# One DMA queue for the stores, and row loads issued a step ahead, in a projection, RWKV-7 and FFN kernel

## The chip, the cores and the metric

The kernel runs on one core of one Trainium2 chip. The metric is the device time of an execution in microseconds, as the median of several runs. The engines are named as the profile names them: PE (matmul), PEld (weight load, beside PE), DVE (vector), ACT (scalar), POOL (GpSimd) and SP (sync, which only issues transfers here). SPq, ACTq and POOLq are the sequencers of these engines where they issue transfers.

## The reference, cut to what matters

One layer over 2048 frames of width 1024, all in float32:

```
h = rms_norm(x);  z = h @ w_in                        # 3328 columns
y_conv = b * conv3(c * x_in)                          # from 12 x 128 columns of z
y_rwkv = rwkv7(token_shift_lerp(z[rwkv columns]))     # 8 heads of 64, chunks of 64 frames
x = x + concat(y_conv, y_rwkv) @ w_out
x = x + (silu(gate) * val) @ w_down                   # gate, val: conv3(rms_norm(x) @ w_up) + bias
e = rms_norm(p @ w_proj)
x = x + sigmoid(rms_norm(x) @ w_gate) * e
out = rms_norm(x)
```

## The kernel before, in words

Features lie on the partitions and time on the free axis. The 2048 frames are worked in four groups of 512. Every product is split in float32r parts (hi and lo of the rows, hi and lo of the weights) and takes three matmuls of 128x512 for each block of 128 features.

The dense stream has two parts. First come the input projections of all four groups (`in_proj`): for each group 14 products whose results go through the token-shift lerp to a DRAM tensor `zs`, then 12 for the convolution mixer, whose results go to `ys`. After that, each group goes through `dense_rest`: the output projection (`w_out`, tiles `whlo`), up projections in pairs with their convolution (`whlu`, `uf`, `th`), down projections (`ps_d`), the embedding of `p` (`ple_embed`, results to DRAM as `es`), and eight gate products (`whlg`), each of which reads one row of `es` back (`e`). While a group is in its convolution mixer, rows `x` of the next group are loaded and split; in its gate products, rows `y` of the next group are.

Beside the dense stream runs `rwkv`, a generator over 16 units of 128 frames. `drive` takes one step of it for about each half product of the dense stream, so its matmuls lie between the dense ones. A unit first loads its inputs from `zs` (`rwkv_load`: k, tw, ad, gd, v, r). In its middle it sends a block matrix through DRAM (`ltt` to `ld` to `lm`), solves a triangular system on DVE (`pd`, `xs`), and sends the result through DRAM again (`xs` to `xd` to `dt`), from which DVE makes `dn` and POOL fills `tT`. At its end it stores `yt` to `ys`.

Weights are loaded raw in the first pass only (SP loads, tile `raw` with four buffers, split by ACT and POOL, kept in DRAM by an SP store); in later passes POOL loads the split form. Rows from DRAM go through staging tiles with tag `s` (three buffers). Most results of 128x512 share tag `b` (`buf`, six buffers), which a store holds until it has landed.

PE keeps the order of the program. On the other engines a scheduler lists the instructions, and each engine then works through its list in order: an instruction or a transfer that waits holds up all behind it.

Of the kernel before, what the change touches and what calls it, by code (L numbers as in the profile page):

```python
# [24 lines left out]
R_POST = 3  # L25
R_SCORE = 3
# [4 lines left out]
WRAW = 4  # L31
WHL = 4
NBUF = 6
NLD = 3
# [28 lines left out]
def tile_trunk(  # L63
# [226 lines left out]
    def in_row(pools, g, rows, k):  # L290
        with tc.high_priority():
            x = staged(pools, xT[k, :, g * G : (g + 1) * G], "x")
        rows.add(pools, x, v("mix_norm_g", k))

    def in_proj(pools, g, rows, nxt):
# [18 lines left out]
        for i in range(4):  # L314
# [17 lines left out]
            def evac_b(ps, rstd):  # L332
                u = buf(pools, "yc")
                nc.vector.tensor_tensor(out=u, in0=ps, in1=rstd, op=ALU.mult)
                nc.vector.tensor_tensor(out=u, in0=u, in1=st["c"], op=ALU.mult)
                nc.scalar.dma_start(out=ys[g][:, i, :], in_=u)
# [11 lines left out]
    def ple_rows(pools, g):  # L348
        hs = []
        with tc.high_priority():  # L350
            for k in range(2):
                hi, lo = pair(pools)
                t = staged(pools, pT[k, :, g * G : (g + 1) * G], "p")
# [25 lines left out]
    def out_row(pools, g, rows, k):  # L379
        rows.ss = None  # L380
        with tc.high_priority():
            hi, lo = pair(pools)
            t = staged(pools, ys[g][:, k, :], "y")
# [3 lines left out]
    def dense_rest(pools, g, yrows, nxt):  # L387
# [77 lines left out]
        for first in range(0, NFF, NB):  # L465
            acts = []
            for i in range(first, min(first + NB, NFF)):
                if i == first + 2 and prev is not None:
                    yield from down(first - NB, prev)
                yield from act_pair(i, acts)  # L470
                if i == PLE_AT - 1:
                    prows = ple_rows(pools, g)
# [10 lines left out]
        re = embed[g]  # L483
        for m in range(KD):
# [22 lines left out]
            for _ in product(pools, w, rows3, evac):  # L507
                yield SLOW

        def finish():  # L510
            rstd = ss.rstd(pools)
            with tc.high_priority():
                for m in range(KD):
# [5 lines left out]
                    nc.scalar.dma_start(out=out[m, :, gs], in_=t)  # L519
# [33 lines left out]
    def rwkv_load(rp, S, u):  # L553
# [14 lines left out]
        nc.sync.dma_start(out=r_t, in_=zs[g][:, 0:4, ts])  # L568
        kkv = v("rwkv_k_k", 0, 4)[:, :, None].broadcast_to([P, 4, P])
# [5 lines left out]
        return r_t, k_t, v_t, gd, kr, sq  # L575

    def rwkv_unit(rp, S, u, loaded, following):
# [188 lines left out]
        for pq in range(4):  # L766
            q = pq % 2
            nc.scalar.dma_start(
# [4 lines left out]
        for r in range(4):  # L773
            eng = nc.sync if r % 2 else nc.scalar
# [33 lines left out]
        for pq in range(4):  # L808
            eng = nc.sync if pq % 2 else nc.scalar
# [19 lines left out]
        yield from rest(WAIT - R_BONUS)  # L829
# [101 lines left out]
        nc.scalar.dma_start(out=ys[g][:, 4:8, ts], in_=yt)  # L931
# [18 lines left out]
    def rwkv():  # L950
        following = [None]
        for u in range(4 * NG):
            loaded = following[0] or rwkv_load(rp, S, u)
# [6 lines left out]

    def in_next(g):
        def run(k):
            if g < NG and k < KD:
                in_row(pools, g, rows["in", g], k)
# [24 lines left out]
    for k in range(KD):  # L989
# [11 lines left out]
    for k in range(KD):  # L1001
# [72 lines left out]
```

## Time and profile before

| | |
|---|---|
| median of 3 runs | 2907.62 us (2907.26 to 2908.49) |
| the profiled execution | 2908.45 us |
| its span | 2906.5 us |
| PE busy | 2768.1 us (95%) |
| DVE, POOL, ACT busy | 1908.3, 1117.4 and 959.9 us |
| mean granted clock of PE | 0.984 |

The span is the time from the first to the last instruction of the profiled execution; about 2 us of its time lie outside. Matmuls overlap their neighbours, so that a busy PE is not a PE without loss; idle PE time is loss for certain.

### The profile page before, as it was taken

How to read it: one execution, taken by the hardware profiler on the slowest of the kernel's cores; microseconds unless marked ns; L12 is line 12 of the kernel's file. 1: busy time of each engine (PE TensorE's matmuls, PEld its weight loads, DVE VectorE, ACT ScalarE, POOL GpSimd, SP SyncE). 2: the span in 40 equal slices, each digit the busy share in tenths (PEclk: the TensorE clock that was granted, in tenths of full speed). 3: DMA queues.
4: the chain of work that ended last, by engine and by line, in shares of the span. 5: the costliest groups of instructions: out<-in, count | busy, mean ns of one | idle time of the engine just before them, and what ended most of it. 6: DMA issues, size and time to landing. Idle time of an engine off the chain costs nothing.

```text
span 2906.5 us, 42153 instructions
## 1 busy us (share of the span) xinstructions
PE 2768.1 (95%) x15464; PEld 2226.7 (77%) x15464; DVE 1908.3 (66%) x3039; ACT 959.9 (33%) x1721; POOL 1117.4 (38%) x1700
## 2 busy tenths in 40 slices
PE   8999999999889999989999999999999999999997
PEld 5778888778677877767778887777788877788885
DVE  5575665648587868796766676857676765544446
ACT  5332232312553433443412223434222143411113
POOL 4533232324556565652333333333333332433221
PEclk9999999999999999989999999999999999999998
DMA  8887777767777777767666565766565668666665
GB/s 298 297 261 217 236 214 223 209 210 243 263 252 245 258 241 247 248 228 230 178 186 185 173 192 172 233 202 200 174 192 169 187 187 266 216 195 189 196 188 169
DMA packets 285802, 629.95 MB, mean 217 GB/s; under 512 B 60186, under 2 KB 113690, under 8 KB 285596
## 3 DMA queue, kind: packets, MB, share of 16 engines
q0 software_dynamic: 95040, 346.07, 39.4%
q1 hardware_dynamic: 134144, 232.83, 24.0%
q10 hardware_dynamic: 56412, 48.36, 5.2%
q8 instruction: 122, 2.00, 0.3%
q14 instruction: 84, 0.69, 0.1%
HBM read 467.77 MB, written 159.38 MB: 216 GB/s over the span
## 4 chain that ended last, share of the span: by engine, by line
PE 50%; DVE 22%; DMA 14%; issue 6%; ACT 5%; POOL 3%; ACTq 1%; SPq 0%; DVEq 0%; POOLq 0%
PE ps_mm L86 33%; PE ps_d L86 11%; DVE uf L417 3%; DVE pd L794 3%; DVE xs L798 2%; DMA lm<-ld 1%; DMA xd<-xs 1%; DMA ld<-ltt 1%; DVE zb L255 1%; DVE sq L229 1%; DMA es<-e 1%; PE o_ps L86 1%; DMA dt<-xd 1%; DVE lo L215 1%; DMA x<-in_xT 1%
## 5 line engine op out<-in xcount | busy, mean ns | idle before, releaser
L86 PE MATMUL ps_mm<-hi,whlu 128*128 128x512 f32 x2816 | 910.6, 397 | 11.3 <-POOL whlu L154 5.1
L86 PEld LDWEIGHTS ps_mm<-hi,whlu 128*128 128x128 f32 x2816 | 532.3, 189 | 131.9 <-POOL whlu L154 7.8
L86 PE MATMUL ps_mm<-hi,whlin 128*128 128x512 f32 x1664 | 542.9, 400 | 19.6 <-ACT whlin L153 7.1
L86 PE MATMUL ps_mm<-lo,whlu 128*128 128x512 f32 x1408 | 552.3, 392 | 1.5 <-DVE lo L215 1.5
L86 PE MATMUL ps_d<-hi,whld 128*128 128x512 f32 x1408 | 456.1, 396 | 16.7 <-DMA whld<-kd 7.2
L86 PEld LDWEIGHTS ps_mm<-hi,whlin 128*128 128x128 f32 x1664 | 316.7, 190 | 93.0 <-ACT whlin L153 7.1
L417 DVE SCALAR_TENSOR_TENSOR uf<-zb,vec,uf 128x512 f32<-128x512 f32 x352 | 298.6, 851 | 89.6 <-ACT uf L412 78.4
L86 PE MATMUL ps_mm<-lo,whlin 128*128 128x512 f32 x832 | 328.9, 395 | 2.8 <-DVE lo L215 2.8
L412 ACT ACTIVATE uf<-zb,vec 128x512 f32<-128x512 f32 x176 | 143.1, 815 | 562.0 <-DVE zb L255 536.8
L86 PEld LDWEIGHTS ps_d<-hi,whld 128*128 128x128 f32 x1408 | 265.6, 189 | 79.2 <-DVE x L457 8.4
L86 PEld LDWEIGHTS ps_mm<-lo,whlu 128*128 128x128 f32 x1408 | 266.8, 189 | 56.2 <-DVE lo L215 2.4
L161 POOL DMA_DIRECT2D whlu<-ku x264 | 141.7, 537 | 436.8 <-PE ps_mm L86 289.1
L255 DVE TENSOR_TENSOR zb<-ps_mm,rstd 128x512 f32<-128x512 f32 x216 | 148.5, 688 | 208.0 <-PE ps_mm L86 204.4
L86 PE MATMUL ps_d<-lo,whld 128*128 128x512 f32 x704 | 275.4, 391 | 0.0
L457 DVE TENSOR_TENSOR x<-ps_d,x 128x512 f32<-128x512 f32 x192 | 131.6, 687 | 139.5 <-PE ps_d L86 138.7
L86 PEld LDWEIGHTS ps_mm<-lo,whlin 128*128 128x128 f32 x832 | 158.4, 190 | 38.1 <-DVE lo L215 6.6
L161 POOL DMA_DIRECT2D whlin<-kin x156 | 84.1, 539 | 248.9 <-PE ps_mm L86 207.7
L86 PE MATMUL ps_mm<-hi,whlg 128*128 128x512 f32 x512 | 169.2, 406 | 3.4 <-DMA whlg<-kg 3.4
L86 PE MATMUL ps_mm<-hi,whlo 128*128 128x512 f32 x512 | 163.1, 397 | 8.5 <-DMA whlo<-ko 4.9
L154 POOL TENSOR_TENSOR lo<-th,hi 128x512 fp32r<-128x512 f32 x88 | 115.2, 1310 | 110.9 <-ACT hi L153 110.3
L154 POOL TENSOR_TENSOR whlu<-rawu,whlu 128x512 fp32r<-128x512 f32 x88 | 122.6, 1398 | 88.9 <-ACT whlu L153 79.2
L86 PEld LDWEIGHTS ps_d<-lo,whld 128*128 128x128 f32 x704 | 133.2, 189 | 26.0
(205 smaller groups left out, 4248.0 us busy)
## 6 DMA issues: line engine op xcount, KB each, us to landing
whlu<-ku POOLq DMA_DIRECT2D x264, 512.0 KB, 4.5
whlin<-kin POOLq DMA_DIRECT2D x156, 512.0 KB, 4.8
whld<-kd POOLq DMA_DIRECT2D x132, 512.0 KB, 4.0
ku<-whlu SPq DMA_DIRECT2D x88, 512.0 KB, 4.7
kin<-whlin SPq DMA_DIRECT2D x52, 512.0 KB, 5.3
whlo<-ko POOLq DMA_DIRECT2D x48, 512.0 KB, 5.5
whlg<-kg POOLq DMA_DIRECT2D x48, 512.0 KB, 3.9
rawu<-in_w_up SPq DMA_DIRECT2D x88, 256.0 KB, 4.1
```

Source lines behind the costliest of these rows:

```text
L86: return pin(nc.tensor.matmul(*args, **kw))
L154: nc.gpsimd.tensor_tensor(out=lo, in0=raw, in1=hi.bitcast(F32), op=ALU.subtract)
L161: nc.gpsimd.dma_start(out=t, in_=kept[key])
L215: nc.vector.scalar_tensor_tensor(out=lo, in0=src, scalar=gcol, in1=hi.bitcast(F32), op0=ALU.mult, op1=ALU.subtract)
L229: nc.vector.tensor_tensor(out=sq, in0=sq, in1=self.acc, op=ALU.add)
L255: nc.vector.tensor_tensor(out=zb[:, 2 : G + 2], in0=ps, in1=rstd, op=ALU.mult)
L412: nc.scalar.activation(u, zb[:, 2 : G + 2], AF.Identity, bias=v("ffn_conv_b", n), scale=v("ffn_conv_w", 88 + n),)
L417: nc.vector.scalar_tensor_tensor(out=u, in0=zb[:, d : d + G], scalar=v("ffn_conv_w", 44 * d + n), in1=u, op0=ALU.mult, op1=ALU.add,)
L457: nc.vector.tensor_tensor(out=x2[m], in0=ps, in1=x2[m], op=ALU.add)
L794: tt(out=pd[:, :, :, 0:n], in0=xs[:, :, None, 0:n].broadcast_to([P, 8, 2, n]), in1=lm[:, None, i : i + 2, 0:n].broadcast_to([P, 8, 2, n]), ...
L798: nc.vector.tensor_reduce(out=xs[:, :, i : i + 2], in_=pd[:, :, :, 0:n], op=ALU.add, axis=mybir.AxisListType.X,)
```

## The change

All stores that ACT issued (`zs`, `ys`, `es`, `out`, `ld`) and its halves of `lm` and `dt` are issued by SP: 280 transfers. The load of a row is split from its first use, which comes one call of `nxt` later (`x`, `y`), one feed-forward pair later (`p`), or half a product later (`e`). `rwkv_load` only issues loads; `rwkv_first` holds the first operations and stands six steps later. Unit 0 starts two steps later. There are four staging tiles, and three raw weight tiles where there were four.

```diff
 R_POST = 3
+R_LOAD = 6
...
-WRAW = 4
+WRAW = 3
...
-NLD = 3
+NLD = 4
...
-    def in_row(pools, g, rows, k):
+    def in_load(pools, g, k):
         with tc.high_priority():
-            x = staged(pools, xT[k, :, g * G : (g + 1) * G], "x")
+            return staged(pools, xT[k, :, g * G : (g + 1) * G], "x")
+
+    def in_row(pools, rows, k, x):
         rows.add(pools, x, v("mix_norm_g", k))
...
-                nc.scalar.dma_start(out=zs[g][:, j, :], in_=u)
+                nc.sync.dma_start(out=zs[g][:, j, :], in_=u)
...
-                    nc.scalar.dma_start(out=es[g][:, m, :], in_=t)
+                    nc.sync.dma_start(out=es[g][:, m, :], in_=t)
...
+        ahead = e_load(0)
         for m in range(KD):
             nxt(m)
             w = weight(pools, w_gate[m], f"g{m}")
+            e = ahead
             with tc.high_priority():
-                e = staged(pools, es[g][:, m, :], "e")
                 nc.vector.tensor_tensor(out=e, in0=e, in1=re, op=ALU.mult)
...
+            steps = product(pools, w, rows3, evac)
+            next(steps)
+            yield SLOW
+            if m + 1 < KD:
+                ahead = e_load(m + 1)
+            for _ in steps:
                 yield SLOW
+        nxt(KD)
...
-            nc.scalar.dma_start(
+            nc.sync.dma_start(
                 out=ld[pq].rearrange("c a i j -> i c a j"),
...
-            eng = nc.sync if r % 2 else nc.scalar
+            eng = nc.sync
...
-            eng = nc.sync if pq % 2 else nc.scalar
+            eng = nc.sync
...
-        yield from rest(WAIT - R_BONUS)
+        yield from rest(R_LOAD)
+        if following[0]:
+            rwkv_first(S, following[0])
+        yield from rest(WAIT - R_BONUS - R_LOAD)
...
     def rwkv():
-        following = [None]
+        following = [rwkv_load(rp, S, 0)]
+        yield from rest(R_BONUS)
+        rwkv_first(S, following[0])
+        yield from rest(R_BONUS)
...
         def run(k):
             if g < NG:
-                while k >= 4 and marks["done"] < 4 * g + 3:
-                    next(side, None)
-                out_row(pools, g, rows["out", g], k)
+                if k < KD:
+                    while k >= 4 and marks["done"] < 4 * g + 3:
+                        next(side, None)
+                    loads["out", g, k] = out_load(pools, g, k)
+                if k:
+                    out_row(pools, rows["out", g], k - 1, loads.pop(("out", g, k - 1)))
```

How the lists of the engines move at three places. First ACT in the embedding of group 1's `p`, where `e` is a product's result, `sq` its square, and `tw`, `s` and `tha` are the RWKV unit's. Before:

```order
L370 COPY e<-ps_e 128x512
L619 ACTIVATE tha_13168<-ps_a 128x512
L227 ACTIVATE sq<-e 128x512
L371 DMA es_103<-e 128x512
L370 COPY e<-ps_e 128x512
L572 ACTIVATE tw_144<-tw_144 64x128
L227 ACTIVATE sq<-e 128x512
L371 DMA es_103<-e 128x512
L370 COPY e<-ps_e 128x512
L227 ACTIVATE sq<-e 128x512
```

The same place after the change:

```order
L376 COPY e<-ps_e 128x512
L228 ACTIVATE sq<-e 128x512
L376 COPY e<-ps_e 128x512
L228 ACTIVATE sq<-e 128x512
L376 COPY e<-ps_e 128x512
L639 ACTIVATE s_13216<-ps_s 128x512
L228 ACTIVATE sq<-e 128x512
L645 ACTIVATE tha_13224<-ps_a 128x512
L599 ACTIVATE tw_144<-tw_144 64x128
L661 COPY nrd_13252<-ksum_13248 64x4 x4
```

The stores are gone from ACT, and the unit's `tha` and `tw` stand behind all eight `e` instead of among them; `tw` still comes right behind `tha`.

Second SP at the end of the gate products of group 0 and the start of group 1's output projection (`xr` are its residual rows, `kg` stores of kept weights). Before:

```order
L203 DMA e<-es_102 128x512
L171 DMA kg_1_12205<-whlg_1_12200 128x1024
L203 DMA y<-ys_99 128x512
L203 DMA e<-es_102 128x512
L171 DMA kg_0_12254<-whlg_0_12249 128x1024
L203 DMA y<-ys_99 128x512
L775 DMA lm_12036<-ld_12029 32x1024 x2
L203 DMA e<-es_102 128x512
L171 DMA kg_1_12261<-whlg_1_12256 128x1024
L203 DMA xr<-in_xT 128x512 x8
```

After:

```order
L204 DMA e<-es_102 128x512
L204 DMA y<-ys_99 128x512
L172 DMA kg_0_12247<-whlg_0_12242 128x1024
L172 DMA kg_1_12254<-whlg_1_12249 128x1024
L204 DMA e<-es_102 128x512
L204 DMA y<-ys_99 128x512
L204 DMA xr<-in_xT 128x512
L794 DMA ld_12117<-ltt_12118 32x8x32 x4
L204 DMA xr<-in_xT 128x512 x2
L801 DMA lm_12124<-ld_12117 32x1024 x4
L204 DMA xr<-in_xT 128x512 x3
L541 DMA out<-o 128x512 x5
```

The last `e` and `y` come ahead of the unit's `lm`; `ld` and all four `lm` now stand among the residual rows, and the output stores of the group before behind six of them.

Third SP in the lerp products of group 2, which fill `zs_96`. Before, SP had only the unit's transfers there:

```order
L564 DMA tw_144<-zs_95 64x128
L565 DMA ad_146<-zs_95 64x128
L566 DMA gd_5097<-zs_95 128x128
L203 DMA y<-ys_98 128x512
L563 DMA k_5093<-zs_95 128x4x128
L567 DMA v_5094<-zs_95 128x4x128
L568 DMA r_5092<-zs_95 128x4x128
L775 DMA lm_5018<-ld_5011 32x1024 x2
L803 DMA xd_5079<-xs_5029 128x256
L810 DMA dt_5081<-xd_5079 32x8x32 x2
```

After, for the unit at this place:

```order
L588 DMA gd_3918<-zs_94 128x128
L311 DMA zs_96<-u 128x512
L585 DMA k_3914<-zs_94 128x4x128
L589 DMA v_3915<-zs_94 128x4x128
L590 DMA r_3913<-zs_94 128x4x128
L311 DMA zs_96<-u 128x512 x3
L794 DMA ld_3832<-ltt_3833 32x8x32 x4
L801 DMA lm_3839<-ld_3832 32x1024 x3
L311 DMA zs_96<-u 128x512
L801 DMA lm_3839<-ld_3832 32x1024
L311 DMA zs_96<-u 128x512 x4
L829 DMA xd_3900<-xs_3850 128x256
```

The stores of the lerp results stand behind the unit's `ld` and `lm`, each of which waits for the step before it.

## Rows read from the trace of the kernel before

**Rows 1.** The page: span, busy time of PE, granted clock in 40 slices.
```profile
span 2906.5 us, 42153 instructions
...
PE 2768.1 (95%) x15464; PEld 2226.7 (77%) x15464; DVE 1908.3 (66%) x3039; ACT 959.9 (33%) x1721; POOL 1117.4 (38%) x1700
...
PEclk9999999999999999989999999999999999999998
```
**Rows 2.** Windows, PE alone: stretch, length, busy (instructions), clock, DMA share, GB/s.
```profile
100.00:120.00 20.00, 15.90 (x78) 0.91 0.70 246
...
755.00:1205.00 450.00, 419.86 (x2556) 0.98 0.72 247
1205.00:1312.00 107.00, 93.01 (x470) 0.89 0.68 225
...
1400.00:1425.00 25.00, 22.51 (x108) 0.93 0.80 240
...
1800.00:1906.00 106.00, 100.25 (x461) 0.97 0.76 241
...
1965.00:1985.00 20.00, 16.92 (x83) 0.91 0.85 258
...
2365.00:2445.00 80.00, 74.70 (x313) 0.96 0.76 234
...
2530.00:2840.00 310.00, 309.17 (x1365) 1.00 0.65 193
2840.00:2907.00 67.00, 47.13 (x198) 0.88 0.50 158
```
**Rows 3.** Timeline of PE at the first RWKV unit; in brackets idle time and releaser.
```profile
109.88 0.66 PE L89 MATMUL ps_n<-c_sq,sq 128*128 128x128 f32 x4 [2.04 <-ACT sq L571]
112.59 1.09 PE L89 MATMUL ps_v<-c_sq,v 128*128 128x128 f32 x4 [2.05 <-DMA v<-zs]
```
**Rows 4.** Timeline of ACT, POOL and PE at the end of group 0's gate products.
```profile
1294.52 0.62 ACT L153 CAST hi<-y 128x512 fp32r<-128x512 f32 x1 [3.20 <-DMA ld<-ltt]
...
1295.22 1.28 POOL L154 TENSOR_TENSOR lo<-y,hi 128x512 fp32r<-128x512 f32 x1 [2.05 <-ACT hi L153]
...
1296.46 1.10 POOL L161 DMA_DIRECT2D whlo<-ko  x2
...
1305.18 0.79 PE L86 MATMUL ps_mm<-hi,whlo 128*128 128x512 f32 x1 [4.45 <-DMA whlo<-ko]
```
**Rows 5.** Timeline of PE at the end of group 2's gate products.
```profile
2413.96 0.80 PE L86 MATMUL ps_mm<-hi,whlg 128*128 128x512 f32 x1 [3.44 <-DMA whlg<-kg]
```
**Rows 6.** Timeline of ACT and PE in the embedding of group 1.
```profile
1410.95 0.31 ACT L572 ACTIVATE tw<-tw 64x128 f32<-64x128 f32 x1 [2.58 <-DMA tw<-zs]
...
1414.53 1.13 PE L86 MATMUL ps_g<-gd,gup 128*128 128x128 f32 x8 [2.49 <-DVE suv L655]
```
**Rows 7.** Timeline of ACT and DVE around one unit's `dt`.
```profile
1348.53 0.38 ACTq L810 DMA_DIRECT2D dt<-xd  x1
1349.01 0.63 ACT L227 ACTIVATE sq<-x 128x512 f32<-128x512 f32 x1 [4.14 <-DMA xd<-xs]
...
1349.68 0.69 DVE L229 TENSOR_TENSOR sq<-sq 128x512 f32<-128x512 f32 x1 [3.42 <-ACT sq L227]
```
**Rows 8.** One line's instructions each: count, time of an issue in ns (min/median/max).
```profile
L775 ACTq DMA_DIRECT2D lm<-ld x32: 456/493/950, 157.8 to 2280.3; - x32
...
L810 ACTq DMA_DIRECT2D dt<-xd x32: 309/384/782, 202.3 to 2320.2; - x32
```
**Rows 9.** Transfers by line: engine, count, size, median us from issue to landing.
```profile
zs<-u ACTq DMA_DIRECT2D x56, 256.0 KB, 4.8
```
**Rows 10.** Waits: us in total, times, longest.
```profile
DVE dn L814 <- DMA dt<-xd: 67.6, 16, 8.2
...
DVE fold L783 <- DMA lm<-ld: 41.2, 11, 7.1
...
PE ps_mm L86 <- POOL whlu L154: 5.1, 6, 1.4
```

More of the change, by code (lines that the diff above doesn't have):

```diff
@@ L335, in evac_b @@
                 nc.vector.tensor_tensor(out=u, in0=u, in1=st["c"], op=ALU.mult)
-                nc.scalar.dma_start(out=ys[g][:, i, :], in_=u)
+                nc.sync.dma_start(out=ys[g][:, i, :], in_=u)
             if i:
@@ L346, in in_proj, with ple_load, ple_rows @@
             yield from project(4 + i, evac_b)
-    def ple_rows(pools, g):
+    def ple_load(pools, g):
+        with tc.high_priority():
+            return [staged(pools, pT[k, :, g * G : (g + 1) * G], "p") for k in range(2)]
+    def ple_rows(pools, ts):
         hs = []
         with tc.high_priority():
-            for k in range(2):
+            for t in ts:
                 hi, lo = pair(pools)
-                t = staged(pools, pT[k, :, g * G : (g + 1) * G], "p")
                 residual(t, hi, lo)
@@ L377, in tile_trunk, with out_load, out_row @@
     pending, embed = [], {}
-    def out_row(pools, g, rows, k):
+    def out_load(pools, g, k):
+        with tc.high_priority():
+            return staged(pools, ys[g][:, k, :], "y")
+    def out_row(pools, rows, k, t):
         rows.ss = None
@@ L382, in out_row @@
             hi, lo = pair(pools)
-            t = staged(pools, ys[g][:, k, :], "y")
             residual(t, hi, lo)
@@ L470, in dense_rest @@
                 yield from act_pair(i, acts)
+                if i == PLE_AT - 2:
+                    pload = ple_load(pools, g)
                 if i == PLE_AT - 1:
-                    prows = ple_rows(pools, g)
+                    prows = ple_rows(pools, pload)
                 if i == PLE_AT:
@@ L483, in dense_rest, with e_load @@
         re = embed[g]
+        def e_load(m):
+            with tc.high_priority():
+                return staged(pools, es[g][:, m, :], "e")
+        ahead = e_load(0)
         for m in range(KD):
@@ L505, in evac @@
                     ss.add(pools, x2[m])
-            for _ in product(pools, w, rows3, evac):
+            steps = product(pools, w, rows3, evac)
[4 more added lines that the diff above has]
+            for _ in steps:
                 yield SLOW
+        nxt(KD)
         def finish():
@@ L518, in finish @@
                     )
-                    nc.scalar.dma_start(out=out[m, :, gs], in_=t)
+                    nc.sync.dma_start(out=out[m, :, gs], in_=t)
         pending.append(finish)
@@ L568, in rwkv_load, with rwkv_first @@
         nc.sync.dma_start(out=r_t, in_=zs[g][:, 0:4, ts])
+        return r_t, k_t, v_t, gd, kr, sq
+    def rwkv_first(S, loaded):
+        r_t, k_t, v_t, gd, kr, sq = loaded
+        tw = S["tw"][0]
         kkv = v("rwkv_k_k", 0, 4)[:, :, None].broadcast_to([P, 4, P])
@@ L930, in rwkv_unit @@
         hi_tt(out=yt, in0=yt, in1=g_t, op=ALU.mult)
-        nc.scalar.dma_start(out=ys[g][:, 4:8, ts], in_=yt)
+        nc.sync.dma_start(out=ys[g][:, 4:8, ts], in_=yt)
         yield
@@ L950, in rwkv @@
     def rwkv():
-        following = [None]
+        following = [rwkv_load(rp, S, 0)]
+        yield from rest(R_BONUS)
+        rwkv_first(S, following[0])
+        yield from rest(R_BONUS)
         for u in range(4 * NG):
-            loaded = following[0] or rwkv_load(rp, S, u)
+            loaded = following[0]
             following[0] = None
@@ L959, in tile_trunk @@
     rows = {(kind, g): Rows() for kind in ("in", "out") for g in range(NG)}
+    loads = {}
     def in_next(g):
         def run(k):
-            if g < NG and k < KD:
-                in_row(pools, g, rows["in", g], k)
+            if g < NG:
+                if k < KD:
+                    loads["in", g, k] = in_load(pools, g, k)
+                if k:
+                    in_row(pools, rows["in", g], k - 1, loads.pop(("in", g, k - 1)))
         return run
@@ L987, in all_in @@
             yield from in_proj(pools, g, rows["in", g], in_next(g + 1))
-    for k in range(KD):
+    for k in range(KD + 1):
         in_next(0)(k)
@@ L1000, in tile_trunk @@
     drive(stream)
-    for k in range(KD):
+    for k in range(KD + 1):
         out_next(0)(k)
```

3 lines of the change are left out of this document (2 added, 1 removed).

## The prediction, made before the changed kernel was run

> **What bounds the kernel now.** The page comes first: PE is busy 2768.1 us of a span of 2906.5, and at full clock in nearly every slice [rows 1]. So PE carries the time, and 2906.5 - 2768.1 = 138.4 us of it PE stands idle. The second view is the table of windows, PE alone, cut by stage [rows 2]. Its stretch from 2530 to 2840, in which no RWKV work is left, shows what a full PE looks like: 309.17 of 310 us busy, clock 1.00, 1365 matmuls, hence 0.2265 us for each. The reader is to look for stretches that fall short of this, in busy time and in clock. A clock of 0.91 over 20 us means that part of the stretch ran at 1.2 GHz where 2.4 is full speed; I price it as (1 - clock) x length, since that work would have taken half as long. The loss so priced comes on top of idle time, and in these rows it stands in stretches that also hold idle time. Third come timelines around the largest holes, to see what each ended on [rows 3 to 7]. The engines beside PE are half idle on average; they matter where one of them stands in its list with work behind it that PE needs.
>
> **What the change removes.** I go by stage, idle time plus clock.
>
> The first RWKV unit [rows 2, 3]. From 100 to 120 us PE is busy 15.90 of 20, idle 4.1, and loses 20 x 0.09 = 1.8 by the clock: 5.9. Both holes wait for the unit's inputs (`k` through its square: 2.04; `v`: 2.05). The unit now starts two steps later, which is two half products of 12 matmuls, 24 x 0.2265 = 5.4 us, and the inputs are 4.1 us late. That leaves 1.3 us for stores of `zs` that stand in SP's list a little. Ends: 0 and 5.9; I take 5, near the upper, as the margin is positive.
>
> The gate products and the start of the next group's output projection [rows 2]. The stretches 1205 to 1312, 1800 to 1906 and 2365 to 2445 are idle for 13.99 + 5.75 + 5.30 = 25.0 us and lose 107 x 0.11 + 106 x 0.03 + 80 x 0.04 = 18.2 us by the clock, 43.2 in all. Here rows `y` are loaded for immediate use. ACT stands for the row or for `ld`, which it must see landed before it issues `lm` (3.20); POOL stands behind ACT for `lo` (2.05); behind that `lo` in POOL's list are the weight loads `whlo`, and PE then waits 4.45 for one [rows 4]. At the end of group 2 the same chain costs 3.44 [rows 5]. With the load a product earlier the row lies there when ACT comes to it, and the issue of `lm` is no longer ACT's. These two holes are 7.9 of the 25.0 us, and the same share of the clock loss is 5.7: together 13.6. Of the other 29.6 us I take a quarter, 7.4, because `e` and the splitting of rows stand in the same lists of DVE and ACT. Sum 21; ends 8 and 43.
>
> The embedding of `p`, 1400 to 1425 and 1965 to 1985 [rows 2]: idle 2.49 + 3.08, by the clock 25 x 0.07 + 20 x 0.09 = 3.5, sum 9.1. ACT stands 2.58 us in front of `tw` for its load, with `e` rows behind it, DVE is late behind ACT, and `ps_g` waits 2.49 [rows 6]. In the new list all eight `e` come before `tw`; but `tw` still follows `tha` at once, so that ACT will stand there again, with less behind it. I take 6; ends 0 and 9.
>
> The first pass of the up and down projections, 755 to 1205: idle 30.1, by the clock 450 x 0.02 = 9.0 [rows 2]. What the change takes away there is ACT standing for transfers. One unit shows the size: ACT stands 4.14 us until `xd` has landed, and DVE behind it 3.42 [rows 7]; for `ld` 3.20 [rows 4]. Three units lie in the stretch, 3 x (4.14 + 3.20) = 22 us of standing, most of which PE does not feel. Ends 0 and 22; I take 5, nearer the lower, since PE lost only 30.1 of 450 us there to all causes. The issues themselves (0.3 to 0.5 us each [rows 8]) are on an engine that is busy for 960 of 2906.5 us [rows 1] and are worth nothing by themselves.
>
> The tail after 2840, where PE is busy 47.13 of 67 [rows 2], is mostly the last norm and the last stores, which stay; an earlier last `e` is worth perhaps 1. Gains: 5 + 21 + 6 + 5 + 1 = 38 us.
>
> **What it adds.** The four `lm` and four `dt` of a unit were issued two by two on SP and ACT, and now one after the other: 2 x 0.493 + 2 x 0.384 = 1.75 us more per unit [rows 8], 28 us over 16 units, on a chain for which DVE already stands 67.6 + 41.2 us [rows 10]. PE idles 138 us where DVE idles 2906.5 - 1908.3 = 998 [rows 1], a seventh; by that share 28 costs 4. Ends 0 and 28. Three raw weight tiles in place of four shorten the reach of the weight loads in the first pass. PE waits 5.1 us for `whlu` now [rows 10]. Tiles of split weights stand between the raw ones and PE, so I add 3; ends 0 and 15 (three times 5.1). Stores that land later hold tiles of tag `b` longer; I add 1 and give the rest to a rival. Costs: 8.
>
> Sum: 38 - 8 = 30 us off the profiled execution's 2908.45, which is 0.8 above the median; so 2877.6 against the median's 2907.62. I say **2878 us**.
>
> **A rule weighed.** The transfers by line show stores that land 4.8 us after issue [rows 9], and ACT that stands before it can issue the next link of a chain [rows 7]. The Trainium skill, in "DMA: Bandwidth & Descriptors", section "Issuing engines are not separate DMA queues", says that issuing from several engines saves only the sequencer's time, usually small. By it the move to one queue should be nearly free, as my 4 us have it. But the same page, section "Anatomy of one DMA — SWDGE (gpsimd) path", says that DMA engines never wait on semaphores, and that a wait is served on the issuing sequencer before dispatch. The trace agrees (4.14 us of ACT [rows 7]). By that rule the standing does not vanish; it moves into SP's list, and that speaks against this change: it is the first rival.
>
> **The rivals.**
> *SP becomes the place that stands (slower).* In the lerp products of groups 1 to 3, stores of `zs` now come behind `ld`, `lm` and `dt`, and each of these waits for a landing or for DVE. If a store is late, its tile of tag `b` is held, the next evacuation waits for a tile, and PE for a free result bank. If the whole stand of 4.14 us [rows 7] reached PE once per unit, it would cost 16 x 4.14 = 66, against 38 of gain: 2908 + 28 = about 2936. It decides from 38 / 16 = 2.4 us per unit. Against it: a lerp result comes every 24 matmuls, 5.4 us, and its store lands after 4.8, so one or two of six tiles are held; a store that is late by 8 us holds two more. For it: the new list has up to five stores behind `lm`, and convolution stages hold more tiles. Chance 0.13.
>
> *The holes are hidden or filled again.* If the list of DVE and not the loads is what makes PE wait, each hole comes back elsewhere: DVE has the same work, and its waits for `dn` and `fold` stay [rows 10]. The change also does less than it says: `tw` still stands right behind `tha`. Only the first unit (5) and the two holes that end on a row (7.9 and 5.7) are then gained, less 8: 2908 - 11 = about 2897, or nothing at all where the costs are twice as large: about 2905. Chance 0.17, of which 0.10 is within 0.2%.
>
> *Freed ACT empties DVE's list as well.* Half of the gate stretches' 43 (21 more is the most; I take 15), 15 of the 22 in the first pass and little cost: 2908 - 60 = about 2848. For it speaks that DVE's stand of 3.42 is ACT's [rows 7]. Against it, that DVE is busy 1908 us whatever ACT does. Chance 0.08.
>
> **How the numbers follow.** The forecast holds 0.62, for 2852 to 2894. The faster rivals reach 2848 and below, the slower one 2936. A measurement tells about 0.2% (5.8 us) from no change. Faster: 0.62 + 0.08 + 0.07 = 0.77; within: 0.10; slower: 0.13. The range 2846 to 2904 leaves out the slower rival, half of no change and a little at the fast end, some 0.2. It takes in all bounds except 28 for the serial issues together with 15 for the raw tiles.
>
> **What would show each step.** Right: no hole in front of `ps_n` and `ps_v` of the first unit; the clock of 1290 to 1312 near 1.00 and no wait of ACT's `hi` for `y`; no ACT wait that ends on `xd` or `ld`; PE idle near 110 us. Wrong: PE waits for `whlu` of over 10 us in the first pass; SP standing tens of us with stores behind it, and evacuations that wait for `zs` or `ys` to land; new holes in front of up projections where DVE stands for `dn`. The prediction is wrong as a whole if PE idle time stays near 138 us although the loads no longer show as waits: then DVE's list was the cause.

## The result, and the profile after the change

The changed kernel takes 2928.58 us (median of 3, 2927.70 to 2934.06) where the kernel before takes 2907.62: the ratio is 1.007, 95% interval 1.0046 to 1.0093. It is 0.7% slower, and 2878 was forecast. The profiled execution is the longest of the three (its span is 2931.8 us), so that the trace shows 25.3 us more than [rows 1], of which 21 are the median's. First the page: span, busy time, and the granted clock in 40 slices.

```profile
span 2931.8 us, 42183 instructions
...
PE 2768.9 (94%) x15464; PEld 2224.9 (76%) x15464; DVE 1908.2 (65%) x3039; ACT 960.5 (33%) x1721; POOL 1107.1 (38%) x1700
...
PEclk9999999999999999999999999999999999999998
```

PE is busy for as long as before (2768.9 against 2768.1), so the 25 us are idle PE: 2931.8 - 2768.9 = 162.9, where it was 138.4. The first thing to look at is where the loss sits. Each dense product ends in one evacuation on DVE, and both traces have as many of them, so the n-th of one can be paired with the n-th of the other. The difference of their end times, taken at the stage boundaries of the prediction (times of the kernel before), gives what each stretch of the program gained or lost in us, here for the changed kernel and for some of the experiments told below. One execution stands behind each row, and two kernels that differ little can differ by 10 us in one stretch (345 to 745 above all), so entries under some 4 us say little by themselves. A profiled execution need not lie at its kernel's median either: that of split_noshift took 2920.46 us where the median is 2932.71, that of w3_catch 2884.53 where it is 2893.59.

```
from us          0     24    124    345    745   1200   1330   1800   1930   2365   2480   2840
changed       -3.8   -3.8   +2.2   +8.5   +1.2   +7.2   +0.6   +5.4   +5.3   +2.6   +0.7   -0.9
before_shift  -1.2   -3.9   +2.6  +10.5   -3.7   +6.7   -5.0   +5.5   -2.6   -1.1   -0.2   -0.2
q_split       +0.2   +2.2   +3.2  +13.8   -0.8   -0.8   -5.0   -0.0   +1.0   +2.2   -0.3   -0.9
split_noshift -3.0   +0.0   +0.2  +13.7   +2.8   -1.3   -2.9   -1.0   +1.2   +2.8   +0.5   -1.0
lmdt_split    -3.4   -3.9   -1.2   +1.8   +2.0   +7.3   -5.2   +6.7   -0.1   +0.8   +0.7   -1.0
split_first0  -3.6   -3.6   +0.8  +12.5   +2.9   +6.4   -3.5   +5.2   +0.1   +1.1   +0.3   -1.0
loads_only    -3.1   -3.9   +5.2  +12.5   +6.2   +7.7   -1.1   +7.1   -2.4   -1.5   +0.6   -0.7
loads_noshift -2.5   +0.0   +0.8   +0.5   -2.9   -1.1   -1.0   -3.3   -1.6   +3.4   +0.7   -1.0
w3_catch      -3.2   -3.6   -2.7   -0.3   -2.0   +0.1   -5.9   -4.2   -1.7   -0.1   +0.9   -1.0
```

In the changed kernel the first unit gains 3.8 of the 5 us that were forecast (24 to 124). The window that answers to the first of [rows 2] is full, with the clock at 2.4 GHz throughout:

```profile
100.00:120.00 20.00, 19.93 (x102) 1.00 0.86 300
```

The gate products of groups 0 and 1 (from 1200 and 1800), where the gain was to come from, lose 7.2 and 5.4. Four kinds of loss follow, each shown by its rows (start, us, engine, operation, in brackets idle time and releaser); they do not make up the whole of it.

**lm behind one issuer.** A down projection of group 1:

```profile
1467.55 2.01 SPq L794 DMA_DIRECT2D ld<-ltt  x4
1473.23 2.39 SPq L801 DMA_DIRECT2D lm<-ld  x4
...
1480.74 0.69 DVE L809 TENSOR_TENSOR fold<-lm,c_sq 128x512 f32<-128x512 f32 x1 [7.70 <-DMA lm<-ld]
1481.35 0.69 DVE L439 SCALAR_TENSOR_TENSOR th<-th,uf 128x512 f32<-128x512 f32 x1
1481.95 0.75 DVE L426 SCALAR_TENSOR_TENSOR uf<-zb,vec,uf 128x512 f32<-128x512 f32 x1
1482.62 0.68 DVE L466 TENSOR_TENSOR x<-ps_d,x 128x512 f32<-128x512 f32 x1
...
1483.35 0.79 PE L87 MATMUL ps_d<-hi,whld 128*128 128x512 f32 x1 [6.41 <-DVE x L466]
```

The reader is to see the order on DVE: `fold` stands 7.70 us for `lm`, and behind it in the list is `x`, the evacuation that frees a result bank. PE waits 6.41 for that. All four `lm` take 2.39 us to issue; over 16 units the time from the first issue to the end of the last is 41.7 us, and was 25.7. The same hole stands once more in front of 2051.52 (6.93). The one issuer is only a part of its cause: in loads_only (below), where `lm` is issued by two engines and every queue is as before, the first of these holes is 7.26 us.

**dt behind one issuer.** First pass, group 0's output projection, POOL:

```profile
740.03 0.39 POOL L847 COPY tt<-dt 32x256 f32<-32x256 f32 x1 [2.56 <-DMA dt<-xd]
741.93 0.39 POOL L847 COPY tt<-dt 32x256 f32<-32x256 f32 x1 [1.51 <-DMA dt<-xd]
744.30 0.84 POOL L847 COPY tt<-dt 32x256 f32<-32x256 f32 x2 [1.98 <-DMA dt<-xd]
745.22 2.94 POOL L155 TENSOR_TENSOR whlo<-rawo,whlo 128x512 fp32r<-128x512 f32 x2
...
746.54 0.76 PE L87 MATMUL ps_mm<-hi,whlo 128*128 128x512 f32 x1 [4.49 <-POOL whlo L155]
```

The four `dt` land one after the other, POOL takes them one by one, and the split of a weight that PE needs stands behind them. In front of 339.84 it is loads of weights for the input projections (`whlin`) that stand in POOL's list behind its waits for `dt`, and PE waits 2.96 for one of them. PE's waits for `whlin` loads are 14.1 us in the whole run, where they were 4.3.

**The end of a unit in the gate products.** Group 0, first DVE before, then DVE and PE after:

```profile
1222.78 0.68 DVE L590 TENSOR_TENSOR on<-on,gr 128x512 f32<-128x512 f32 x1
...
1240.46 1.75 DVE L216 SCALAR_TENSOR_TENSOR lo<-x,vec,hi 128x512 fp32r<-128x512 f32 x1
1242.14 1.75 DVE L616 TENSOR_TENSOR on<-on,gr 128x512 f32<-128x512 f32 x1
...
1243.94 1.11 PE L90 MATMUL ps_y<-c_sq,on 128*128 128x128 f32 x4 [6.40 <-DVE on L616]
```

No transfer is waited for. DVE works without a pause from 1228 to 1246 (the last rows `x` of the group, their squares and splits), and `on`, the unit's last step, is listed among them, while PE has come to the unit's `ps_y` already. Units two steps later meet this crowd; before, `on` was done at 1222.78, and PE waited 1.9 us for an `on` in the whole run, where it now waits 10.3.

**Rows ahead that are not ahead.** The end of group 2's gate products:

```profile
2425.83 1.29 POOL L155 TENSOR_TENSOR lo<-y,hi 128x512 fp32r<-128x512 f32 x1 [3.07 <-ACT hi L154]
2427.14 0.32 SPq L204 DMA_DIRECT2D y<-ys  x1
2430.68 0.62 ACT L154 CAST hi<-y 128x512 fp32r<-128x512 f32 x1 [4.40 <-DMA y<-ys]
2431.38 1.29 POOL L155 TENSOR_TENSOR lo<-y,hi 128x512 fp32r<-128x512 f32 x1 [3.21 <-ACT hi L154]
2432.70 0.32 SPq L204 DMA_DIRECT2D y<-ys  x1
2435.94 0.62 ACT L154 CAST hi<-y 128x512 fp32r<-128x512 f32 x1 [3.59 <-DMA y<-ys]
```

The load of a row starts 0.02 us after `lo` of the row before has ended (2425.83 + 1.29 = 2427.12): that is when a staging tile comes free. SP's own waits agree: it stands 125.4 us, 24 times, for `lo` in front of a row load (92.6 us, 25 times, before). Each of these loads waits for the row just before it, so that the fourth tile puts no row in reserve here. ACT stands 4.40 and 3.59 us for the rows, where it stood 4.31 and 4.68 before. The waits by line say so for the whole run; before:

```profile
ACT hi L214 <- DMA x<-in_xT: 60.9, 15, 7.2
ACT hi L153 <- DMA y<-ys: 29.4, 11, 4.9
DVE e L489 <- DMA e<-es: 16.6, 12, 4.3
```

After (beside the lines of [rows 10]):

```profile
ACT hi L215 <- DMA x<-in_xT: 77.7, 16, 16.7
DVE dn L840 <- DMA dt<-xd: 59.9, 15, 6.0
DVE fold L809 <- DMA lm<-ld: 45.1, 9, 8.4
ACT hi L154 <- DMA y<-ys: 29.8, 12, 5.2
DVE e L505 <- DMA e<-es: 24.7, 9, 5.9
```

In these lines rows x, y and e are waited for 132.2 us in all, where it was 106.9.

### The profile page after: what moved, and what is told of

Read it like the earlier page. It is cut to its first block, busy times and chain, and to the rows that moved or that the text cites. A ratio compares the mean times of both kernels' runs of the same rounds, so it can differ in the third digit from the quotient of the medians.

```text
span 2931.8 us, 42183 instructions
## 1 busy us (share of the span) xinstructions
PE 2768.9 (94%) x15464; PEld 2224.9 (76%) x15464; DVE 1908.2 (65%) x3039; ACT 960.5 (33%) x1721; POOL 1107.1 (38%) x1700
## 4 chain that ended last, share of the span: by engine, by line
PE 36%; DVE 13%; DMA 7%; issue 4%; ACT 3%; POOL 1%; SPq 1%; DVEq 0%; POOLq 0%; ACTq 0%
PE ps_mm L87 21%; PE ps_d L87 12%; DVE uf L426 2%; DVE pd L820 1%; DMA lm<-ld 1%; DMA y<-ys 1%; DVE xs L824 1%; DVE zb L256 1%; DMA ld<-ltt 1%; DVE sq L230 1%; DVE x L466 1%; DMA out<-o 1%; DMA dt<-xd 1%; DMA whlu<-ku 1%; DVE th L439 1%
## 5 line engine op out<-in xcount | busy, mean ns | idle before, releaser
L87 PE MATMUL ps_mm<-hi,whlin 128*128 128x512 f32 x1664 | 543.8, 401 | 24.4 <-DMA whlin<-kin 14.1
L426 DVE SCALAR_TENSOR_TENSOR uf<-zb,vec,uf 128x512 f32<-128x512 f32 x352 | 305.2, 869 | 97.2 <-ACT uf L421 88.1
```

The source lines that it names most:

```text
L87: return pin(nc.tensor.matmul(*args, **kw))
L426: nc.vector.scalar_tensor_tensor(out=u, in0=zb[:, d : d + G], scalar=v("ffn_conv_w", 44 * d + n), in1=u, op0=ALU.mult, op1=ALU.add,)
```

## The experiments

They ran on four chips, each against the kernel before on its own chip. There the kernel before spread over 10 to 23 us in 18 to 35 runs (on one: 2898.99 to 2921.26 in 19), so ratios of medians are given with their 95% intervals. Two versions are often compared across chips, each by its own ratio; a difference of two ratios is uncertain by some 0.2 to 0.3%, and one below that is called not clear of noise. "Changed" is the changed kernel. The letters are those of the theories in the expectations.

**What the queue costs.** q_only: before, with all 280 transfers on SP.

```diff
-nc.scalar.dma_start(out=zs[g][:, j, :], in_=u)      # also ys, es, out, ld
+nc.sync.dma_start(out=zs[g][:, j, :], in_=u)
-eng = nc.sync if r % 2 else nc.scalar               # lm; dt alike
+eng = nc.sync
```

> The kernel before with one part of the change alone: all 280 transfers that ACT issued go to SP; loads, units and pools as before. Theory A (the one queue is the cost: lm issued one after the other arrives late at fold, with evacuations behind it in the list of DVE): slower than before by 12 to 30 us, 2920 to 2938, with PE waiting for x behind fold. Theory B (the shift of the units and of their first operations re-orders DVE's list, and that is the cost): within 5 us of before, 2903 to 2912. Theory C (three raw tiles in place of four): as B.

Measured: 1.0052 (1.0034 to 1.0071). A's time holds, at the lower end: the queue alone makes it slower. A's sign does not: PE waits 2.1 us for an `x` of the down projections, and waited 4.0 before. What has grown is its wait for `ps_g`, 19.4 us where it was 11.1.

q_split: the same, with halves of `lm` and `dt` on ACT as before (the last pair of lines left out).

> The kernel before with stores and ld on SP, and lm and dt in halves on SP and ACT as before. Theory A1 (the serial lm and dt alone made the version with everything on SP 0.5% slower): within 4 us of before. Theory A2 (stores behind the unit's waits in SP's list are the cost): 8 to 15 us slower than before.

Measured: 1.0030 (1.0018 to 1.0042). A2 holds at its lower end: stores and `ld` behind each other on SP are 0.30%, or 8.7 us. For serial `lm` and `dt` the difference to q_only leaves 0.22%, which is no larger than its own uncertainty. The table puts the cost of the stores into the projections of groups 1 to 3 (+13.8 from 345). By the same pairing all five versions with the units at their old place and stores on SP lose some 10 to 14 us there (q_only, noshift and q_split_tw are the others), and the four with stores on ACT lose at most 5. The timeline there, ACT before, then SP, ACT and PE in q_split:

```profile
386.28 0.31 ACT L572 ACTIVATE tw<-tw 64x128 f32<-64x128 f32 x1 [0.97 <-DMA tw<-zs]
...
386.54 1.00 SPq L308 DMA_DIRECT2D zs<-u  x2
389.24 0.37 SPq L931 DMA_DIRECT2D ys<-yt  x1
389.70 0.47 SPq L564 DMA_DIRECT2D tw<-zs  x1
...
396.11 0.31 ACT L572 ACTIVATE tw<-tw 64x128 f32<-64x128 f32 x1 [6.58 <-DMA tw<-zs]
...
399.90 1.41 PE L86 MATMUL ps_g<-gd,gup 128*128 128x128 f32 x5 [3.84 <-DVE suv L655]
```

The load of the next unit's `tw` is issued behind a `ys` store for whose data SP stands 1.6 us. It then lands 6.4 us after its issue, where it took 3.9 at the same place before. For both together ACT stands 6.58 us (0.97 before), and PE 3.84.

lmdt_split: the changed kernel with halves of `lm` and `dt` on ACT.

```diff
-            eng = nc.sync
+            eng = nc.sync if r % 2 else nc.scalar     # lm; dt alike
```

> The changed kernel with only the halves of lm and dt on ACT again; stores and ld stay on SP. Theory A: fold comes some 1 to 4 us earlier per unit and the two holes of 6.4 and 6.9 us in front of ps_d go: 2914 to 2922. Theories B and C: within 4 us of the changed kernel, 2924 to 2932.

Measured: 1.0028 (1.0015 to 1.0041), against 1.007 with all on SP: 0.42% or 12 us, the time of A. A's sign came by half: the two holes in front of `ps_d` are smaller (4.10 and 5.02, were 6.41 and 6.93), but they did not go. `fold` stands 3.04 where it stood 7.70, so 4.66 us less on DVE gave PE 2.31:

```profile
1467.52 0.69 DVE L809 TENSOR_TENSOR fold<-lm,c_sq 128x512 f32<-128x512 f32 x1 [3.04 <-DMA lm<-ld]
...
1470.13 0.50 PE L87 MATMUL ps_d<-hi,whld 128*128 128x512 f32 x1 [4.10 <-DVE x L466]
```

loads_only: changed, with every transfer back on its old queue.

```diff
-nc.sync.dma_start(out=zs[g][:, j, :], in_=u)        # also ys, es, out, ld
+nc.scalar.dma_start(out=zs[g][:, j, :], in_=u)      # and lm, dt in halves
```

> The changed kernel with its queues undone: stores, ld and halves of lm and dt on ACT again; row loads ahead, the later first operations, the later start of unit 0 and the pools stay. Theory A: faster than before, 2885 to 2902, since what remains are the loads ahead. Theory B: slower than before by 10 to 25, 2918 to 2933. Theory C: slower, with PE waiting for whlu and whlin over 10 us more than before.

Measured: 1.0072 (1.0053 to 1.0090). A's own figure is missed by far: without the queue the kernel is as slow as with it, as B says. So something else in the change costs as much, and the parts do not add up. The hole behind `fold` is there too, with `lm` issued by two engines:

```profile
1492.78 0.69 DVE L809 TENSOR_TENSOR fold<-lm,c_sq 128x512 f32<-128x512 f32 x1 [4.63 <-DMA lm<-ld]
...
1495.39 0.80 PE L87 MATMUL ps_d<-hi,whld 128*128 128x512 f32 x1 [7.26 <-DVE x L466]
```

**The units' place.** noshift and split_noshift: changed and lmdt_split, with unit 0 at its old place.

```diff
         following = [rwkv_load(rp, S, 0)]
-        yield from rest(R_BONUS)
         rwkv_first(S, following[0])
-        yield from rest(R_BONUS)
```

> The changed kernel with unit 0 at the place that it had before (load and first operations at once, no two steps between), so that each unit meets the dense stages as it did. Theory B: most of the loss goes, 2905 to 2916. Theories A and C: the loss stays and the first unit's holes of 4 to 8 us return: 2928 to 2938.

> The changed kernel with halves of lm and dt on ACT again and unit 0 at its old place. Theory B1: the hole in front of ps_y goes and group 0's gate stage is as before, the first unit's holes of 4 to 7 us are back; against the version with halves alone (0.28% slower than before) 0 to 5 us faster, 0.1 to 0.3% slower than before. Theory D: as slow as before that or slower, by 4 to 8 us.

Measured: 1.0072 (1.0048 to 1.0097) and 1.0061 (1.0042 to 1.0081); on the sum A and C are right in noshift (the loss stays), and D in split_noshift (as slow as lmdt_split, or slower by 4 to 8 us; it is 9.6 slower, uncertain by 7); B and B1 missed. The stages of split_noshift tell why: the gate products lose nothing now (-1.3, -1.0), as B1 says, but the projections of groups 1 to 3 lose 13.7, with the holes of q_split in front of `ps_g`. With stores on SP the later place avoids the one and meets the other. Between these two, serial `lm` and `dt` make 0.11%, not clear of noise.

before_shift: before, with unit 0 two steps later and nothing else.

```diff
-        following = [None]
+        following = [rwkv_load(rp, S, 0)]
+        yield from rest(2)
```

> The kernel before with unit 0 started two steps later and nothing else: every unit meets the dense stages two half products later. Theory B1 (the place at which a unit's end and start fall in the gate products decides: the hole of 6.4 us in front of ps_y at the start of group 0's gate products comes from there): the first unit gains 5 to 7 us, group 0's gate stage loses 8 to 10, the sum is within 5 us of before or up to 8 slower, and that hole is in the trace. Theory D (the row loads ahead make that hole, as e and its splits move in DVE's list): no such hole, 4 to 8 us faster than before.

Measured: 0.9997 (0.9986 to 1.0007), with the hole in front of `ps_y`:

```profile
1243.96 1.12 PE L89 MATMUL ps_y<-c_sq,on 128*128 128x128 f32 x4 [6.38 <-DVE on L590]
```

B1 holds, with smaller sizes: 6.7 and 5.5 us lost in the gate products come with the place alone, with no row loaded ahead, and the first unit's 3.9 are gained. The rest comes back in other stretches, and the time is that of the kernel before.

loads_noshift: loads_only with unit 0 at its old place (rows ahead, first operations later and pools remain).

> The changed kernel with all queues as before and unit 0 at its old place: what remains is rows ahead, the first operations six steps later, and the pools. With the units later, this was 0.72% slower than before. Theory J (the units' place costs, rows and first operations don't): 0.25% faster to 0.1% slower than before, no holes in front of ps_y, gate products of groups 0 and 1 within 2 us of before. Theory K (first operations later cost once ACT also issues stores, as ACT then meets them together): 0.3 to 0.8% slower.

Measured: 0.9993 (0.9982 to 1.0003), J. Beside loads_only only the place differs: 0.79% (on two chips). DVE does `on` of the unit above at 1218.82 in this kernel, ahead of the crowd, and PE has no hole in front of `ps_y`:

```profile
1218.82 0.68 DVE L616 TENSOR_TENSOR on<-on,gr 128x512 f32<-128x512 f32 x1
```

PE's waits in the whole run, in us, put the place beside the queues: for `x` in front of `ps_d`, for `on` in front of `ps_y`, for `suv` in front of `ps_g`, and for loads of `whlin`. Place is that of the units; "halves" and "one" tell whether two engines issue `lm` and `dt`, or SP alone.

```
                place   stores   lm, dt     x      on     suv   whlin
before          old     ACT      halves    4.0    1.9    11.1     4.3
loads_noshift   old     ACT      halves    4.2    1.9    11.7     2.8
q_split         old     SP       halves    3.7    1.9    17.3     6.1
split_noshift   old     SP       halves    4.3    2.2    17.8     6.3
q_only          old     SP       one       2.1    1.9    19.4     6.0
noshift         old     SP       one       3.7    1.9    21.4     5.6
before_shift    later   ACT      halves    6.4   10.2     7.9    16.3
loads_only      later   ACT      halves   14.1   10.3    10.5    11.1
lmdt_split      later   SP       halves   14.6   10.3     5.5     7.7
changed         later   SP       one      20.0   10.3     5.3    14.1
```

The waits for `on` go with the place alone. Those for `x` need the later place and some other part of the change: serial `lm` at the old place leaves them at 2.1 and 3.7, and before_shift has 6.4. Those for `suv` grow with stores on SP, at the old place only.

**Rows, pools, first operations.** split_norows: lmdt_split with rows loaded where they are used.

```diff
-                    loads["in", g, k] = in_load(pools, g, k)
-                if k:
-                    in_row(pools, rows["in", g], k - 1, loads.pop(("in", g, k - 1)))
+                    in_row(pools, rows["in", g], k, in_load(pools, g, k))   # y, p, e alike
```

> The changed kernel with halves of lm and dt on ACT again and rows x, y, e, p loaded where they are used, as before; the unit's later first operations, its start, the stores on SP and the pools stay. Theory D (row loads ahead cost, since a row taken early moves the work on it forward in the lists): faster than the version with halves alone by 5 to 12 us, near or below before. Theory B1: within 4 us of the version with halves alone, unless the rows bring what was forecast; then slower by up to 13.

Measured: 1.0061 (1.0047 to 1.0075). D falls: without the rows ahead it is 0.33% slower than lmdt_split (on another chip), so here they are worth some 9.5 us.

before_w3: before with the two pool sizes.

```diff
-WRAW = 4
-NLD = 3
+WRAW = 3
+NLD = 4
```

> The kernel before with three raw weight tiles and four staging tiles, nothing else. Theory C (fewer raw tiles make PE wait in the first pass): 5 to 12 us slower than before, with the loss ahead of 1240 us. Theory F (the unit's first operations six steps later are what remains to be explained): within 4 us of before.

Measured: 0.9978 (0.9961 to 0.9994): C falls, and so does my term of 3 us for fewer raw tiles. The pools alone make the kernel faster; which of the two sizes does it was not separated.

split_first0, split_w4 and split_first0_w4: lmdt_split with the first operations right behind the loads, with the old pools, and with both.

```diff
         following[0] = rwkv_load(rp, S, u + 1)
+        if following[0]:
+            rwkv_first(S, following[0])
...
-WRAW = 3
-NLD = 4
+WRAW = 4
+NLD = 3
```

> The changed kernel with halves of lm and dt on ACT again, and each unit's first operations right behind its loads, as before. Theory F: 5 to 10 us faster than the version with halves alone, which was 0.28% slower than before: 0.05% faster to 0.1% slower than before. Theory C: within 4 us of that version, 0.15 to 0.4% slower than before.

> The changed kernel with halves of lm and dt on ACT again, four raw weight tiles and three staging tiles. Theory C: 5 to 10 us faster than the version with halves alone, the gain ahead of 1240 us: 0.05% faster to 0.1% slower than before. Theory F: within 4 us of that version, or slower, as rows loaded ahead need the fourth staging tile.

> Both of these together: what remains of the change are rows x, y, e, p a step ahead, stores and ld on SP, and the later start of unit 0. If the parts add up (stores on SP 8.7 us, rows ahead -9.5, the start 0), it is within 4 us of before whichever of C and F holds. If they don't add up, because each edit gives DVE and ACT another list, it may lie up to 20 us above.

Measured: 1.0026 (1.0012 to 1.0040), 1.0047 (1.0027 to 1.0067) and 1.0041 (1.0022 to 1.0059). In split_first0 F falls: the first operations' place is worth nothing, as the change moved it in the program and not in the list (the 16 `tw` stand at the same places of ACT's list in split_first0 and lmdt_split). In split_w4 C falls: the old pools are slower by 0.19% here, the way of before_w3 though not clear of noise. The last one shows once more that the parts don't add.

**The stand of tw.** q_split_tw, w3_tw, rows_tw and split_tw: q_split, before_w3, before_w3 with rows ahead, and lmdt_split, each with a tile of its own for the raw `tw`, so that its load is issued when the unit before has read it.

```diff
+        twr = rp["prep"].tile([64, P], F32, tag="twr", name=f"twr{u}")
-        nc.sync.dma_start(out=tw[0:64, :], in_=zs[g][0:64, 12, ts])
+        nc.sync.dma_start(out=twr, in_=zs[g][0:64, 12, ts])
-        nc.scalar.activation(tw[0:64, :], tw[0:64, :], AF.Tanh)
+        nc.scalar.activation(tw[0:64, :], twr, AF.Tanh)
```

> The kernel before with stores and ld on SP (0.3% slower), and tw loaded into a tile of its own, so that its load is issued a whole unit earlier and ACT finds it there. Theory G (the load of tw behind the stores in SP's list, and ACT in front of it, is what those stores cost): 7 to 15 us faster than without, between 0.2% faster and 0.1% slower than before; the holes of 3 to 4 us in front of ps_g are gone. Theory H (the stores cost elsewhere, or the lists' new order does): 0.2 to 0.4% slower than before.

> The kernel before with the new pools (three raw, four staging tiles; 0.22% faster) and tw in a tile of its own; all queues as before. Theory G: PE's waits for ps_g fall from 11.1 us to under 3; 6 to 12 us faster than the pools alone, 0.4 to 0.65% faster than before. Theory H: within 4 us of the pools alone, 0.1 to 0.35% faster than before.

> The version above and rows x, y, e, p loaded a step ahead; all queues, the units' place and their first operations as before. If rows ahead are worth what the version without them lost (9.5 us with stores on SP): 0.7 to 1.0% faster than before. If they only move work forward in the lists of ACT and DVE: within 0.15% of the version above, or slower.

> The changed kernel with halves of lm and dt on ACT again (0.28% slower than before) and tw in a tile of its own. Theory G: its PE waits for ps_g are 5.5 us, so 2 to 6 us faster, 0.05 to 0.2% slower than before; the holes of the gate products that come from the units' new place (6.4 in front of ps_y) stay. Theory H: no change, 0.2 to 0.35% slower.

Measured: 1.0017 (1.0005 to 1.0029), 0.9978 (0.9964 to 0.9992), 0.9989 (0.9977 to 1.0002), 1.0031 (1.0017 to 1.0045). ACT's stand of 33.0 us in q_split falls to 2.8. That is worth 0.13% there, which is not clear of noise, and nothing elsewhere, as H says of w3_tw and split_tw; `ps_g` is still waited for (15.3 us, was 17.3). G is a part of the cost of the stores at most. Rows ahead, alone on top of the pools, gain nothing: 0.11% slower than w3_tw on the same chip, within noise.

**The gain without the loss.** w3_catch: before_w3, unit 0 two steps later, and its long rest two steps shorter, so that later units keep their place.

```diff
-        yield from rest(WAIT - R_BONUS)
+        yield from rest(WAIT - R_BONUS - (2 if u == 0 else 0))
```

> The kernel before with the new pools, unit 0 two steps later, and unit 0's long rest two steps shorter, so that units 1 to 15 are where they were. Theory J: the first unit gains 4 to 5 us and the gate products of groups 0 and 1 are within 2 us of before: 0.3 to 0.45% faster than before (the pools alone: 0.22% faster). If the list of DVE changes everywhere as soon as one unit moves: 0.1% faster to 0.2% slower.

Measured: 0.9975 (0.9962 to 0.9989), 2893.59 us beside 2902.16 of the kernel before on that chip: the lowest ratio here, beside 0.9978 of the pools alone. It is just short of J's range, with the range inside its interval. The stages agree with J but for a gain in group 1: -3.6 at the first unit, +0.1 and -4.2 in the gate products, and no hole of 6 us in front of `ps_y`. What unit 0 adds to the pools' 0.22% is less than these intervals can tell.

## Why the prediction was wrong

It was wrong in its sign: 30 us less were forecast, and 21 more came. By its steps:

- *PE idle is the loss.* Right: busy time is unchanged, and the result is 24.5 us more of idle PE.
- *The first unit, 5 us.* Right in its mechanism: both holes of [rows 3] are gone, and all six versions of the table with unit 0 later gain 3.6 to 3.9 (24 to 124). That is no more than the idle 4.1; of the 1.8 priced by the clock nothing is seen to come on top, though the clock of 100 to 120 rose from 0.91 to 1.00. But "the unit now starts two steps later" was counted as a gain alone. The step moves all 16 units, and it costs 12.6 us in the gate products of groups 0 and 1 (7.2 + 5.4; 6.7 + 5.5 in before_shift). That DVE's list there is full was in the trace before; the prediction left out what a unit's end would meet.
- *The gate products, 21 us.* This is the step that failed: the three gate stretches lost 7.2 + 5.4 + 2.6 = 15.2 us where 21 were to be gained. I took 13.6 us for two holes that end on a row, as "with the load a product earlier the row lies there when ACT comes to it". At the end of group 2 it doesn't: the staging tile, not the place of the load in the program, sets when the transfer starts. In the whole run ACT waits 29.8 us for rows y, after 29.4 before. At the end of group 2 PE now waits 2.07 and 3.87 for weight loads, where the hole of [rows 5] was 3.44. At the end of group 0 three of the last four rows do lie there when ACT comes, and the hole of [rows 4] is gone; but the row was the smaller part of that hole. POOL stood 2.05 us behind ACT; the `whlo` load that PE waited for then landed 8.68 us after its issue, where the median of such a load is 5.5 (the chain that ended last, and the transfers by line, before):

```profile
1296.46 8.68 DMA whlo<-ko
...
whlo<-ko POOLq DMA_DIRECT2D x48, 512.0 KB, 5.5
```

Where only rows, first operations and pools are changed (loads_noshift), the three gate stretches give -1.1, -3.3 and +3.4, and with the stores on SP too (split_noshift) -1.3, -1.0 and +2.8: nothing in sum. What is lost beyond that came with the units' later place (above).
- *The embedding, 6 us.* Right for the place: its two holes of 2.49 and 3.08 in front of `ps_g` are gone, and PE is busy for 24.33 of 25 us there (1411 to 1436) and 23.34 of 24 (1976 to 2000), at clock 1.00. New holes behind `fold`, in the down projections some 60 us later (6.41, 6.93), took more.
- *Up and down projections in the first pass, 5 us.* 1.2 were lost there. ACT's waits that end on `ld` or `xd`, 39.8 us before, are all gone, so they were off the path, or what they gave was taken elsewhere.
- *Serial lm and dt, 4 us.* Mis-sized for the changed kernel: 12 us (lmdt_split, on another chip). At the old place it is 6 (q_only against q_split) and 3 (noshift against split_noshift), neither clear of noise. The time of issue was counted rightly: from the first issue to the end of the last, over 16 units, `lm` went from 25.7 to 41.7 us and `dt` from 19.0 to 33.4, 30.4 more where 28 were forecast. What failed is scaling it by a seventh, the share of DVE's idle time that PE feels on average. A late `fold` stands at a fixed place in DVE's list: with an evacuation behind it PE waited 20.0 us for `x` in the whole run, and in noshift, where DVE stands even longer for `lm` (50.8 us; 45.1 in the changed kernel), only 3.7. The rule I weighed, by which several issuers save only a little sequencer time (the Trainium skill, "DMA: Bandwidth & Descriptors", section "Issuing engines are not separate DMA queues"), has the size of the saving right: 16.0 us of `lm` issue over 16 units. What that is worth depends on what stands behind the chain.
- *Raw tiles, 3 us of cost.* Wrong sign: together with the fourth staging tile they gain 0.22% (before_w3).
- *Stores, 1 us.* Mis-sized: stores and `ld` on SP cost 0.30% or 9 us in the kernel before. The rival in which SP becomes the place that stands had the sign and 2936 us. The mechanism that I gave, tiles held by late stores, is in the traces but small: in q_split ACT waits 5.1 us for `es` to land before it can evacuate an `e` (3.0 before), and 14.7 for `out` in front of a square (8.2 before). Loads of the next unit that stand behind the stores are another part; removing that stand for `tw` gave back 0.13 of the 0.30%, not clear of noise. So most of the cost is not named.

What stays open: why the parts don't add. The units' later place costs 0.79% with rows ahead on the old queues (loads_only against loads_noshift), nothing in the kernel before, and is a gain of 0.33% with stores on SP (lmdt_split against split_noshift); rows ahead gain 0.33% in one setting and nothing in another. One reason can be read from the waits: stores on SP cost at `ps_g` only with the units at their old place, and `fold` meets an evacuation only with the units later, so the two moves do not pay for the same holes. Much of the scatter lies in the projections of groups 1 to 3 (345 to 745). Stores on SP lose 10 to 14 us there at the old place; with the units later it is 2 to 13, in part in front of `whlin` loads, and lmdt_split and split_first0, equally fast, have +1.8 and +12.5. before_shift has +10.5 there and is as fast as the kernel before. That each edit gives the engines another list is seen in the traces; that the lists alone explain it was only argued. Whether more than four staging tiles would bring the rows ahead in time was not tried.

## What to carry to other kernels

A load written a step earlier is earlier only if its tile is free a step earlier: compare the time of the issue with the end of the last reader of the tile, before counting a gain. A wait on an engine with an ordered list costs by what stands behind it at that place, so price a longer chain by the instruction behind it and not by the engine's average idle time. Here splitting the links of such a chain over two issuers was worth 12 us where an evacuation stood behind it, and nothing clear of noise elsewhere. When a change has several parts, time each alone: here two pool sizes held a gain of 0.22%, and the rest of the change lost more than it.

## What the runs showed of the hardware that was not expected

The same program took different times by chip: the medians of the kernel before are 2902.16, 2910.96, 2913.49 and 2916.02 us on four of them, with a granted clock of 0.98 to 0.99 in all profiled executions. On one chip it spread over 10 us in 18 runs and over 23 in 26 others, so the 1.2 us among the first 3 runs say little of its spread. A 256 KB store took about as long from either issuer: `zs` landed 4.8 us after issue from ACT [rows 9] and 4.5 from SP, `es` 5.2 and 5.5, `out` 6.3 and 6.2. Four loads of 128 KB (`lm`) took 1.38 us to issue from two engines and 2.39 from one.
